# Entry of a two-layer step on one core: norm squares over whole tiles, the order of first loads, and the place of the later modulation groups

## The chip, the cores and the metric

The kernel runs on one core of one Trainium2 chip. TensorE (PE) does the matrix products, ScalarE (ACT) and VectorE (DVE) the elementwise work, GpSimd (POOL) a little of it; SyncE (SP), ACT and POOL issue DMAs. The metric is the device time of one execution in microseconds, lower being better.

## The reference, cut to what matters

Two trunk layers with adaptive layer norm run over 512 latent and 128 context tokens of width 1024. The change lies in the first lines of layer 0: modulation, norm, and the first input projection.

```python
m = jax.nn.silu(cond) @ w_mod + b_mod                      # shift, scale, gate x 2
y = xf * lax.rsqrt(jnp.mean(xf * xf, axis=-1, keepdims=True) + RMS_EPS)
h = y * g * (1.0 + scale) + shift
p = h @ w_in                                               # cq, ckv, krope, nq, nk, nv
cq = rms_norm(cq, q_norm)
```

## The kernel before

Activations lie transposed: eight tiles x[0] to x[7] of 128 x 640, one for each 128 of the width; columns 0 to 319 and 320 to 639 are the left and the right half (a and b in names of results). A product in fp32 precision is made of three fp32r products: the weight's high part with h's high part (h00h), the same with h's residue (h00l), and the weight's residue with h00h. The high part of a weight tile is an ACT copy (L184), its residue a DVE subtraction (L185). So one unit of 128 output rows costs 8 k x 2 halves x 3 = 48 products.

The entry, in the order in which it is written:

- vec (norm gains, biases, conditions) is loaded on SP (L131); ACT makes silu of the conditions (L332, L333) and loads the exponential tables (L159).
- x is loaded by eight DMAs on SP (L495). The class Norm squares each half of each tile on ACT (L211, L214) and adds it up on DVE (L215). rstd sums over partitions with a product against ones (tile n00p) and makes the reciprocal root on ACT.
- fetch(j) loads the weights of modulation group j in two halves of 1 MB (tile mraw, L523); j = 0 to 3 covers the shift and scale of k = 2j and 2j + 1. m[j][0] and m[j][1] are its products (32 in the profile's count, tile mod), m[j][2] a selection (sel, four short products) and the bias add on DVE (L363).
- made(j) does the selection, the gain (gs, L370), and then hm.make for k = 2j and 2j + 1 in both halves: a DVE product (h00t, L241), ACT's high part (h00h, L245), DVE's residue (h00l, L246). The right half is done in two pieces, columns 320 to 511 and 512 to 639, which have different conditions.
- first(ks, us) does the products of units 0, 1 and 2 (weights wA0, wA1, wA4) for some k.

Behind it, lowrank copies the results of units 0 and 1 (cqr) and squares and adds them (cqacc), the tile tabK serves kra and krb on DVE, and wA2 and wA3 give the next unit pair, ckv0 and ckv1. cqp is the norm sum over cqacc on PE. nvp follows with a third kind of products.

Each engine runs its instructions in a fixed order. Program order and a list scheduler at build time set that order; `run` gives each piece the latest product as the point behind which it may be placed. Raw weights pass through three buffers, split weights through three more.

Of the kernel before, what the change touches and what calls it, by code (L numbers as in the profile page):

```python
# [11 lines left out]
F32 = mybir.dt.float32  # L12
F32R = mybir.dt.float32r
AF = mybir.ActivationFunctionType
# [4 lines left out]
P = 128  # L19
D = 1024  # L20
KT = D // P
NS = 512
NP = 128
T = NS + NP
# [26 lines left out]
def body(ctx, tc, xT, vecs, crow, wm0, wm0g, wm1, wA, wNV, wNA, wMK, wMV, wOA, wGQ, wGK, wGV, wOC,  # L51
         wFI, wFO, cckvT, ckrT, cnkT, cnv, cgkT, cgv, rpbp, tabM, tabK, tabG, maskN,
         yT, o_ckvT, o_krT, o_nkT, o_nv, o_gkT, o_gv):
    nc = tc.nc
    V, S, G = nc.vector, nc.scalar, nc.gpsimd

    class PE:

        last = None
# [28 lines left out]
    def bank(name, kind="m"):  # L88
        if kind == "m":
            return psp.tile([P, 512], F32, tag="m", bufs=4, name=name)  # L90
        return ypool["pool"].tile([P, 512], F32, tag=kind, bufs=ypool["tags"][kind], name=name)
# [4 lines left out]
    def pair(name, kind="y"):  # L96
        return [bank(f"{name}a", kind), bank(f"{name}b", kind)]
# [7 lines left out]
    def f(ap):  # L105
        return ap.bitcast(F32)
# [4 lines left out]
    HALF = ((0, HT), (HT, T))  # L111
    HCOND = (((0, HT, 0),), ((HT, NS, 0), (NS, T, 1)))

    def run(pieces):

        for piece in pieces:
            with tc.issue_after(PE.last.ins):
                piece()
# [7 lines left out]
    def named(prefix, pieces):  # L126
        return {f"{prefix}{i}": piece for i, piece in enumerate(pieces)}


    vec = main.tile([P, V_ALL], F32, name="vec")  # L130
    nc.sync.dma_start(vec, vecs)  # L131
    ident = main.tile([P, P], F32, name="ident")
    make_identity(nc, ident)
    ones = main.tile([P, P], F32, name="ones")
# [27 lines left out]
    def load(src, n, name):  # L162
        raw = rawp.tile([P, 1024], F32, tag="raw", name=name)
        nc.sync.dma_start(raw[:, :n], src)
        return raw[:, :n]

    def after(inst, fn):
        if inst is None:
            return fn()
        with tc.issue_after(inst.ins):  # L170
            return fn()
# [3 lines left out]
    def unit(src, n, name, lo="v", pool=None, behind=None, raw=None):  # L175

        if raw is None:
            raw = load(src, n, name + "r")
        elif src is not None:
            nc.sync.dma_start(raw, src)  # L180
        t = (pool or wp).tile([P, 2, 1024], F32R, tag="w", bufs=3, name=name)
        hi, lw = t[:, 0, :n], t[:, 1, :n]
        at = behind if isinstance(behind, tuple) else (behind, behind)
        split[:] = (after(at[0], lambda: S.activation(hi, raw, AF.Copy)),  # L184
                    after(at[1], lambda: (V if lo == "v" else G).tensor_tensor(lw, raw, f(hi), ALU.subtract)))  # L185
        return hi, lw

    def mm3(ps, a, b, h, l, st, sp, **k):
        PE.matmul(ps, a, h, start=st, stop=False, **k)
        PE.matmul(ps, a, l, start=False, stop=False, **k)  # L190
        PE.matmul(ps, b, h, start=False, stop=sp, **k)

    def proj(ps, wh, wl, hh, hl, ks, c0, c1, first=True, last=True, w0=0):

        for j, k in enumerate(ks):
            a, b = wh[:, (w0 + j) * P:(w0 + j + 1) * P], wl[:, (w0 + j) * P:(w0 + j + 1) * P]
            mm3(ps[:, :c1 - c0], a, b, hh[k][:, c0:c1], hl[k][:, c0:c1], first and j == 0, last and j == len(ks) - 1)


    class Norm:  # L200
        last = None
# [165 lines left out]
    def mkgs(l, i, k0=0, k1=8):  # L367
        sc = SC1 if i == 0 else SC2
        n = (V_NMIX if i == 0 else V_NFFN) + 8 * l
        V.scalar_tensor_tensor(gs[l][i][:, k0:k1, :], mods[l][:, sc + k0:sc + k1, :], 1.0, bc2(vec[:, n + k0:n + k1]),  # L370
                               ALU.add, ALU.mult)
# [119 lines left out]
    nrm = Norm("n00", D)  # L491
    x = []
    for k in range(KT):
        xk = ring.tile([P, T], F32, tag="x", name=f"x0_{k}")
        nc.sync.dma_start(xk, xT[:, k, :])  # L495
        x.append(xk)
    for k in range(KT):
        for i in range(2):
            nrm.add(x[k], i)
    hm = Mod("h00", x, gs[0][0], mods[0], SH1, (range(8), range(8)))  # L500
    hh, hl = hm.hh, hm.hl
    cnd = keep.tile([P, 2, KT], F32, name="cnd")
# [5 lines left out]
    nc.gpsimd.dma_start(crs.rearrange("c (k p) -> (c k) p", p=P), cnr[:2 * KT, :])  # L508
    pss = [pair(f"wA{u}") for u in range(2)] + [[bank(f"wA2{c}") for c in range(2)]]

    def first(ks, us):
        for k in ks:
            for u in us:
                for c, (c0, c1) in enumerate(HALF):
                    proj(pss[u][c], *w3[u], hh, hl, [k], c0, c1, first=k == 0, last=k == KT - 1, w0=k)

    with tc.tile_pool(name="start", bufs=1) as big:
        raws = {}

        def fetch(j):  # L520
            for half in range(2):
                raws[j, half] = big.tile([P, 2, 1024], F32, tag="mraw", bufs=8, name=f"mraw{j}_{half}")
                nc.sync.dma_start(raws[j, half], wm0[j, 2 * half:2 * half + 2].rearrange("q p n -> p q n"))  # L523


        fetch(0)
        w3 = [unit(wA[0], 1024, "wA0")]
        fetch(1)
        w3 += [unit(wA[i], 1024, f"wA{i}") for i in (1, 4)]
        fetch(2)  # L530
        fetch(3)
        m = [mod0(j, lambda j=j: bank(f"mod{j}", "m"), lambda j, half: [raws[j, half][:, q, :] for q in range(2)]) for j in range(4)]

        def made(j):

            m[j][2]()
            mkgs(0, 0, 2 * j, 2 * j + 2)
            for k in (2 * j, 2 * j + 1):
                for i in range(2):
                    hm.make(i, nrm.rs, k)  # L540

        def rows(j):
            return m[j][:2]

        nrm.rstd(0)
        run([lambda: nrm.rstd(1)] + rows(0))
        run([lambda: made(0)] + rows(1))
        run([lambda: first((0, 1), [0]), lambda: made(1), lambda: first((0, 1), [1, 2])])
        run(rows(2))
        run([lambda: first((2, 3), [0]), lambda: made(2), lambda: first((2, 3), [1, 2])])  # L550
        run(rows(3))
        run([lambda: first((4, 5), [0]), lambda: made(3), lambda: first((4, 5), [1, 2])])
        run([lambda u=u: first((6, 7), [u]) for u in range(3)])
    sb = ExitStack()
    sa = ExitStack()
    aa = sa.enter_context(tc.tile_pool(name="aa", bufs=1, reuse_waits="tile"))
    ab = sb.enter_context(tc.tile_pool(name="ab", bufs=1, reuse_waits="tile"))

    kr = keep.tile([P, 768], F32, name="kr")
    for q in range(4):  # L560
        nc.scalar.dma_start(kr[32 * q:32 * q + 32, 512:640], ckrT)

    def lowrank(nm, pss):
        ts, nr = [], Norm(nm, 256)
# [47 lines left out]
    pss = [pair(f"ckv{u}") for u in range(2)]  # L612
# [16 lines left out]
    for kk in range(4):  # L629
        wh, wl = wnext  # L630
        for j in range(2):
            k = 2 * kk + j
            a, b = wh[:, 512 * j:512 * (j + 1)], wl[:, 512 * j:512 * (j + 1)]
            for i in range(5):
                c0, c1 = P * i, P * i + P
# [289 lines left out]
    for h in range(8):  # L925
        p, r = divmod(h, 2)
# [8 lines left out]
        qh, ql, ks = [t[r] for t in nqk[p]]  # L935
        pieces = named("s", sc)
# [124 lines left out]
    for h in range(8):  # L1061
        p, r = divmod(h, 2)
# [6 lines left out]
        pieces = named("s", sc)  # L1069
# [758 lines left out]
    x, pend = mixer_out(wOA, oMs + oNs, [4, 5, 6, 7, 0, 1, 2, 3], x_again, mods[0], "oa", nxt, op[-1], begun, scored)  # L1828
# [3 lines left out]
    x, pend = ffn(0, x, pend, box["m"], nxt, side, op)  # L1832


    hh, hl = box2["m"].hh, box2["m"].hl
# [226 lines left out]
    for h in range(8):  # L2062
        oG.append(gp.tile([P, T], F32, tag="go", bufs=8, name=f"oG{h}"))
        pts = []
        pieces = gqa_scores(h, pts)
# [23 lines left out]
    x, pend = mixer_out(wOC, oGs, list(range(8)), lambda n, x=x: x[n], mods[1], "oc", nxt, op[-1], begun, None)  # L2089
# [14 lines left out]
    x, pend = ffn(1, x, pend, box["m"], final, side, op)  # L2104
# [157 lines left out]
```

## Time and profile before

| what | value |
|---|---|
| timed runs | 1481.26, 1482.27 and 1484.97 us, median 1482.27 |
| profiled execution, first to last instruction | 1482.4 us |
| PE busy | 1443.7 us (97%) |
| DVE busy | 1210.9 us (82%) |
| ACT busy | 772.0 us (52%) |
| first product that needs h (wA0) | 24.94 us |
| first product of ckv0a | 53.97 us |
| first product of nvp | 68.89 us |

For the profiled execution the page gives the span alone, 1482.4 us, and no time around it; it lies within the timed runs. In rows of the timeline the first number is the start, the second the length; what follows "<-" in brackets is what ended the idle time before. In the chain of waits each row is a piece of the work that ended last. Windows give pairs of busy time and count for PE, PEld (weight loads), DVE, ACT and POOL, and then the granted clock, the DMA share and GB/s.

### The profile page before, as it was taken

The page shows a single profiled execution, that of the slowest core. Times are in us where ns is not written, and L with a number is a line of the kernel's source. Part 1 is how long each engine was busy: PE and PEld are TensorE (multiplying, and loading weights), DVE is VectorE, ACT ScalarE, POOL GpSimd, SP SyncE. Part 2 cuts the span into 40 slices and gives each one's busy share as a digit, 9 for nine tenths or more (in the row PEclk, how much of TensorE's full clock was granted, in tenths as well). Part 3 has the DMA queues.
Part 4 walks back from the last instruction along what each step waited for, and adds up shares of the span by engine and source line. Part 5 has one row for each costly group of instructions (what it writes and reads, how often), then busy time and mean ns, then how long its engine had stood idle before and what let it go on. Part 6 is the DMA issues. An engine that isn't in the chain of part 4 may idle for free.

```text
span 1482.4 us, 25722 instructions
## 1 busy us (share of the span) xinstructions
PE 1443.7 (97%) x9785; PEld 1394.3 (94%) x9785; DVE 1210.9 (82%) x2278; ACT 772.0 (52%) x1525; POOL 207.0 (14%) x298
## 2 busy tenths in 40 slices
PE   5999989999999999999999999999999999999997
PEld 4988978889999999999999999989999999999996
DVE  5786788886999999977997888775899999954496
ACT  5445677873755444441123666663755555542253
POOL 0226534432000000000001322222000000000000
PEclk9999999999999999999999999999999999999998
DMA  9644511016055555569763211004055556668522
GB/s 368 223 146 138 181 39 43 30 32 211 29 196 171 187 185 183 185 211 344 275 209 128 86 55 46 29 31 135 30 186 177 184 192 206 212 224 308 194 87 72
DMA packets 79900, 228.61 MB, mean 154 GB/s; under 512 B 8864, under 2 KB 14272, under 8 KB 79392
## 3 DMA queue, kind: packets, MB, share of 16 engines
q1 hardware_dynamic: 76832, 219.73, 43.3%
q0 software_dynamic: 1600, 5.14, 1.0%
q10 hardware_dynamic: 1344, 2.10, 0.4%
q8 instruction: 77, 1.26, 0.3%
q14 instruction: 47, 0.39, 0.1%
HBM read 192.23 MB, written 34.69 MB: 153 GB/s over the span
## 4 chain that ended last, share of the span: by engine, by line
PE 83%; DVE 7%; ACT 5%; DMA 2%; issue 2%; POOL 0%; DVEq 0%; ACTq 0%; SPq 0%; POOLq 0%
PE fg L63 21%; PE fd L63 9%; PE fo L63 8%; PE fu L63 6%; PE gq L63 3%; PE nq L63 2%; PE nk L63 2%; PE fo_2b L63 1%; PE fo_0b L63 1%; PE gs L63 1%; PE fo_2a L63 1%; PE fo_0a L63 1%; PE go L63 1%; PE mod L63 1%; PE fo_4b L63 1%
## 5 line engine op out<-in xcount | busy, mean ns | idle before, releaser
L1796 DVE SCALAR_TENSOR_TENSOR junk<-wm,cb 128x1024 bf16<-128x1024 f32 x62 | 75.6, 1220 | 4.6 <-DMA wm<-in_wm 4.1
L1239 ACT ACTIVATE sg<-g 128x320 f32<-128x320 f32 x34 | 16.0, 472 | 114.9 <-DVE g L1239 114.9
L63 PE MATMUL gq<-h10h,wgq 128*128 128x320 f32 x256 | 66.7, 318 | 0.0
L255 POOL TENSOR_SCALAR h10h<-h10t,gs,mods 128x320 fp32r<-128x320 f32 x4 | 3.6, 890 | 429.4 <-DVE h10t L249 427.7
L1239 DVE SCALAR_TENSOR_TENSOR junk<-wm,cb 128x1024 bf16<-128x1024 f32 x50 | 61.0, 1221 | 0.8
L1239 DVE TENSOR_TENSOR wY<-s,wY 128x1024 fp32r<-128x1024 f32 x40 | 48.8, 1220 | 1.1 <-ACT wY L1239 1.0
L1239 DVE TENSOR_TENSOR wZ<-s,wZ 128x1024 fp32r<-128x1024 f32 x40 | 48.8, 1220 | 0.0
L63 PEld LDWEIGHTS gq<-h10h,wgq 128*128 128x128 f32 x256 | 45.0, 188 | 0.9 <-PE gtp L67 0.2
L1239 ACT ACTIVATE wZ<-s 128x1024 fp32r<-128x1024 f32 x40 | 42.4, 1060 | 0.1
L1239 ACT ACTIVATE wY<-s 128x1024 fp32r<-128x1024 f32 x40 | 42.0, 1049 | 0.0
L63 PE MATMUL gq<-h10l,wgq 128*128 128x320 f32 x128 | 39.5, 308 | 0.0
L1978 ACT ACTIVATE gp<-gs,gb,rq 128x640 f32<-128x640 f32 (+1 forms) x40 | 31.9, 797 | 14.5 <-DVE gb L1977 14.1
L63 PE MATMUL fg<-h11E,wW 128*128 128x320 f32 x240 | 38.7, 310 | 0.0
L63 PE MATMUL fg<-h01q,wX 128*128 128x320 f32 x240 | 38.6, 309 | 0.0
L63 PE MATMUL fg<-h11q,wX 128*128 128x320 f32 x240 | 38.6, 309 | 0.0
L63 PE MATMUL fg<-h01N,wZ 128*128 128x320 f32 x240 | 38.6, 309 | 0.0
L63 PE MATMUL fg<-h11N,wZ 128*128 128x320 f32 x240 | 38.6, 309 | 0.0
L63 PE MATMUL fu<-h01q,wX 128*128 128x320 f32 x240 | 38.6, 308 | 0.0
L63 PE MATMUL fu<-h11q,wX 128*128 128x320 f32 x240 | 38.6, 309 | 0.0
L63 PE MATMUL fg<-h01E,wW 128*128 128x320 f32 x240 | 38.6, 309 | 0.0
L63 PE MATMUL fd<-h01q,wZ 128*128 128x320 f32 x240 | 38.5, 309 | 0.0
L63 PE MATMUL fd<-h11q,wZ 128*128 128x320 f32 x240 | 38.5, 309 | 0.0
(3226 smaller groups left out, 5249.6 us busy)
## 6 DMA issues: line engine op xcount, KB each, us to landing
wm<-in_wm SPq DMA_DIRECT2D x48, 512.0 KB, 3.6
mraw<-in_wm SPq DMA_DIRECT2D x8, 1024.0 KB, 15.4
mraw<-in_wm SPq DMA_DIRECT2D x16, 512.0 KB, 3.9
hr_T<-sp_T SPq DMA_DIRECT2D x21, 320.0 KB, 5.9
hr_B<-sp_B SPq DMA_DIRECT2D x18, 320.0 KB, 6.1
mrow<-in_wm0g POOLq DMA_DIRECT2D x8, 512.0 KB, 6.2
wm<-in_wm0g SPq DMA_DIRECT2D x8, 512.0 KB, 3.4
x<-in_xT SPq DMA_DIRECT2D x8, 320.0 KB, 5.7
```

What stands on the lines that cost most here:

```text
L63: cls.last = nc.tensor.matmul(*a, **k)
L255: G.tensor_scalar(h[:, c0:c1], t, self.gsl[:, k, 0:1], self.ml[:, self.sh + k, 0:1], ALU.mult, ALU.add)
L1239: self.last = after(self.last, lambda: op(*a, **k))
L1796: def step(kind, at, line=lambda op, *a, **k: op(*a, **k)):
L1978: weighed.append((S.activation(dst, src, AF.Exp, bias=nb, scale=rq[:, j:j + 1], accum_out=ll[:, j:j + 1]), v))
```

## The change

The diff, with its hunks shortened by nothing but context:

```diff
-    nc.sync.dma_start(vec, vecs)
+    nc.scalar.dma_start(vec, vecs)
+    S.preload_act_table_set("silu_and_others")
...
-    for k in range(KT):
-        for i in range(2):
-            nrm.add(x[k], i)
...
-    def first(ks, us):
+    def first(ks, u):
         for k in ks:
-            for u in us:
-                for c, (c0, c1) in enumerate(HALF):
-                    proj(pss[u][c], *w3[u], hh, hl, [k], c0, c1, first=k == 0, last=k == KT - 1, w0=k)
+            for c, (c0, c1) in enumerate(HALF):
+                proj(pss[u][c], *w3[u], hh, hl, [k], c0, c1, first=k == 0, last=k == KT - 1, w0=k)
...
-        def fetch(j):
+        def fetch(j, half):
+            raws[j, half] = big.tile([P, 2, 1024], F32, tag="mraw", bufs=8, name=f"mraw{j}_{half}")
+            nc.sync.dma_start(raws[j, half], wm0[j, 2 * half:2 * half + 2].rearrange("q p n -> p q n"))
+
+        for k in range(KT - 1):
+            sq = nrm.acc if k == 0 else big.tile([P, T], F32, tag="sq", bufs=2, name=f"n00sq{k}")
+            S.activation(sq, x[k], AF.Square)
+            if k:
+                V.tensor_add(nrm.acc, nrm.acc, sq)
+        nrm.k = [KT - 1, KT - 1]
+        for i in range(2):
+            nrm.add(x[KT - 1], i)
+        for half in range(2):
+            fetch(0, half)
+        w3 = [unit(wA[i], 1024, f"wA{i}") for i in range(2)]
+        for half in range(2):
+            fetch(1, half)
+        w3.append(unit(wA[4], 1024, "wA4"))
+        for j in (2, 3):
             for half in range(2):
-                raws[j, half] = big.tile([P, 2, 1024], F32, tag="mraw", bufs=8, name=f"mraw{j}_{half}")
-                nc.sync.dma_start(raws[j, half], wm0[j, 2 * half:2 * half + 2].rearrange("q p n -> p q n"))
-
-
-        fetch(0)
-        w3 = [unit(wA[0], 1024, "wA0")]
-        fetch(1)
-        w3 += [unit(wA[i], 1024, f"wA{i}") for i in (1, 4)]
-        fetch(2)
-        fetch(3)
+                fetch(j, half)
...
-        def rows(j):
-            return m[j][:2]
-
         nrm.rstd(0)
-        run([lambda: nrm.rstd(1)] + rows(0))
-        run([lambda: made(0)] + rows(1))
-        run([lambda: first((0, 1), [0]), lambda: made(1), lambda: first((0, 1), [1, 2])])
-        run(rows(2))
-        run([lambda: first((2, 3), [0]), lambda: made(2), lambda: first((2, 3), [1, 2])])
-        run(rows(3))
-        run([lambda: first((4, 5), [0]), lambda: made(3), lambda: first((4, 5), [1, 2])])
-        run([lambda u=u: first((6, 7), [u]) for u in range(3)])
+        run([lambda: nrm.rstd(1)] + m[0][:2] + [lambda: made(0)])
+        for j in range(4):
+            k = 2 * j
+            pieces = [lambda: first((k, k + 1), 0), lambda: first((k,), 1), lambda: first((k + 1,), 1), lambda: first((k, k + 1), 2)]
+            if j < 3:
+                pieces[2:2] = [lambda: made(j + 1)]
+                pieces[1:1] = m[j + 1][:2]
+            run(pieces)
...
-    for q in range(4):
-        nc.scalar.dma_start(kr[32 * q:32 * q + 32, 512:640], ckrT)
+    with tc.issue_after(hm.act[KT - 1, 1].ins):
+        for q in range(4):
+            nc.scalar.dma_start(kr[32 * q:32 * q + 32, 512:640], ckrT)
```

The vec load moves to ACT's queue and the table of silu is loaded ahead of its wait. Seven of eight tiles are squared and added whole, the last in halves. The load of wA1 goes ahead of the second modulation group's weights. In each pass the order becomes: unit 0 for both k, the next group's products, unit 1 for the even k, the next group's selection and h, unit 1 for the odd k, unit 2. The four small kr loads go behind the last h on ACT's queue.

How this moves instructions shows at three places. In names, h00h2 is the high part of h for k = 2, h00l2 its residue, wA0a and wA0b the two halves of unit 0, and wA20 and wA21 those of unit 2 (weights wA4).

The first place is PE behind the first modulation group, ahead of the first products with h. Before:

```order
L63 MATMUL mod0_248<-mraw0_1_211,scol_107 32x256 x8
L63 MATMUL mod0_248<-sel_92,modsb0_265 128x4 x2
L63 MATMUL mod1_294<-mraw1_0_218,scol_107 32x256 x8
L63 MATMUL mod1_294<-mraw1_1_220,scol_107 32x256 x8
L63 MATMUL wA0a_200<-h00h0_177,wA0_215 128x320
L63 MATMUL wA0a_200<-h00l0_185,wA0_215 128x320
```

After:

```order
L63 MATMUL mod0_230<-mraw0_1_191,scol_108 32x256 x8
L63 MATMUL mod0_230<-sel_93,modsb0_247 128x4 x2
L63 MATMUL wA0a_157<-h00h0_134,wA0_197 128x320
L63 MATMUL wA0a_157<-h00l0_142,wA0_197 128x320
...
L63 MATMUL wA0b_158<-h00l1_143,wA0_197 128x320
L63 MATMUL wA0b_158<-h00h1_135,wA0_197 128x320
L63 MATMUL mod1_288<-mraw1_0_205,scol_108 32x256 x8
L63 MATMUL mod1_288<-mraw1_1_207,scol_108 32x256 x8
L63 MATMUL wA1a_159<-h00h0_134,wA1_202 128x320
```

The products of modulation group 1 now stand behind all twelve of unit 0 for k = 0 and 1. On DVE, at the same time, the residue of wA1 moves up. DVE before, from the residue of wA0 to that of wA1:

```order
L185 TENSOR_TENSOR wA0_215<-wA0r_213,wA0_215 128x1024
L246 SCALAR_TENSOR_TENSOR h00l0_185<-h00t00_272,mods0_98,h00h0_177 128x320
L241 SCALAR_TENSOR_TENSOR h00t01_276<-x0_0_117,gs00_100,n00rs_116 128x128
L246 SCALAR_TENSOR_TENSOR h00l0_185<-h00t01_276,mods0_98,h00h0_177 128x192
...
L246 SCALAR_TENSOR_TENSOR h00l1_186<-h00t11_287,mods0_98,h00h1_178 128x128
L185 TENSOR_TENSOR wA1_224<-wA1r_222,wA1_224 128x1024
```

After:

```order
L186 TENSOR_TENSOR wA0_197<-wA0r_195,wA0_197 128x1024
L247 SCALAR_TENSOR_TENSOR h00l0_142<-h00t00_254,mods0_99,h00h0_134 128x320
L242 SCALAR_TENSOR_TENSOR h00t01_258<-x0_0_118,gs00_101,n00rs_117 128x128
L186 TENSOR_TENSOR wA1_202<-wA1r_200,wA1_202 128x1024
L247 SCALAR_TENSOR_TENSOR h00l0_142<-h00t01_258,mods0_99,h00h0_134 128x192
```

The residue of wA1 now stands ahead of the right half of k = 0 and of all of k = 1.

The second place is PE between the selection of one group and the first products with its h. Before:

```order
L63 MATMUL mod1_294<-sel_92,modsb1_311 128x4 x2
L63 MATMUL wA1a_202<-h00h0_177,wA1_224 128x320
...
L63 MATMUL wA21_205<-h00h1_178,wA4_229 128x320
L63 MATMUL mod2_376<-mraw2_0_232,scol_107 32x256 x8
L63 MATMUL mod2_376<-mraw2_1_234,scol_107 32x256 x8
L63 MATMUL wA0a_200<-h00h2_179,wA0_215 128x320
```

After:

```order
L63 MATMUL mod1_288<-sel_93,modsb1_305 128x4 x2
L63 MATMUL wA1a_159<-h00h1_135,wA1_202 128x320
...
L63 MATMUL wA21_162<-h00h1_135,wA4_211 128x320
L63 MATMUL wA0a_157<-h00h2_136,wA0_197 128x320
L63 MATMUL wA0b_158<-h00h2_136,wA0_197 128x320
L63 MATMUL wA0a_157<-h00l2_144,wA0_197 128x320
```

Between the selection and h of k = 2 stood 24 products and the next group's 32; now 18 products stand there, and in unit 0 nine of twelve come ahead of the right half of k = 3.

The third place is PE behind the last products of unit 2. Before:

```order
L63 MATMUL wA21_205<-h00l7_192,wA4_229 128x320
L63 MATMUL wA21_205<-h00h7_184,wA4_229 128x320
L63 MATMUL ckv0a_624<-h00h0_177,wA2_614 128x320
L63 MATMUL ckv0a_624<-h00l0_185,wA2_614 128x320
...
L63 MATMUL ckv0a_624<-h00h1_178,wA2_614 128x320
```

After:

```order
L63 MATMUL wA21_162<-h00h7_141,wA4_211 128x320
L63 MATMUL cqp0_706<-cqacc_570,ones_87 128x320
L63 MATMUL ckv0a_606<-h00h0_134,wA2_596 128x320
L63 MATMUL ckv0a_606<-h00l0_142,wA2_596 128x320
L63 MATMUL ckv0b_607<-h00h0_134,wA2_596 128x320
L63 MATMUL ckv0b_607<-h00l0_142,wA2_596 128x320
L63 MATMUL cqp1_712<-cqacc_570,ones_87 128x320
L63 MATMUL ckv1a_608<-h00h0_134,wA3_601 128x320
```

The norm sums cqp moved from behind all of ckv to its front, between products with the high parts of wA2 and wA3. On DVE the residue of wA2 moved behind kra, krb and the cqacc adds, which before it preceded; on ACT the high part of wA2 moved behind all copies and squares of cq.

## The prediction

> **What bounds the kernel now.** I read the page first (span and the chain's shares), then the chain of waits through the entry, then the timeline of each engine there, and last the windows with the granted clock.
>
> ```profile
> span 1482.4 us, 25722 instructions
> PE 83%; DVE 7%; ACT 5%; DMA 2%; issue 2%; POOL 0%; DVEq 0%; ACTq 0%; SPq 0%; POOLq 0%
> ```
>
> PE is on the chain for 83% of the span. Whatever the change does, it does in the first 70 us, and the rest follows as a block as long as PE runs without a gap behind it. The chain there:
>
> ```profile
> 3.08 5.92 DMA x<-in_xT
> 9.02 14.02 DMA mraw<-in_wm
> 23.08 1.94 PE mod L63 x16
> ...
> 26.11 0.80 PE wA0b L63 x3
> ...
> 28.51 0.65 PE mod L63 x4
> ...
> 32.82 1.86 PE mod L63 x32
> ...
> 36.64 0.34 PE mod L63 x4
> ...
> 44.42 0.34 PE mod L63 x4
> ...
> 48.38 0.44 PE wA0a L63 x3
> ...
> 50.05 0.56 PE wA0b L63 x2
> ...
> 52.37 1.76 PE wA L63 x12
> 54.13 3.52 PE ckv0a L63 x24
> ...
> 68.21 1.08 PE cqp L63 x4
> ...
> 104.64 7.05 PE nk L63 x48
> ```
>
> Read from top to bottom: up to 23.08 us the chain waits for DMA (the weights of the second modulation group). From 23.08 to 104.64 + 7.05 = 111.69 us it holds PE alone, so 23.08 us is where the entry ends. Part of what follows ran at half clock:
>
> ```profile
> 22.36:25.77 3.41, 2.69 (x19) 1.43 (x20) 3.41 (x10) 1.78 (x5) 0.66 (x5) 0.50 1.03 412
> 25.77:29.19 3.42, 3.42 (x16) 3.42 (x15) 1.69 (x3) 2.09 (x3) 0.27 (x2) 0.51 1.02 410
> 29.19:54.13 24.94, 24.93 (x206) 22.27 (x207) 17.34 (x49) 12.25 (x30) 3.46 (x11) 1.00 0.60 217
> ```
>
> The last three numbers of a row are granted clock, DMA share and GB/s; the first pair is PE. PE has 24.93 busy of 24.94 us between 29.19 and 54.13: in that stretch nothing is left to gain, only to lose. What can be won lies ahead of 29.19.
>
> **The change part by part.** *1. Start, to the first norm sum on PE.*
>
> ```profile
> 0.74 0.38 SPq L131 DMA_DIRECT2D vec<-in_vecs  x1
> 6.58 5.77 ACT L214 ACTIVATE n00sq<-x 128x320 f32<-128x320 f32 x14
> 8.29 0.67 DVE L144 COPY sel<-ident 32x2 f32<-32x2 f32 x4
> 8.99 4.51 DVE L215 TENSOR_TENSOR n00acc<-n00acc,n00sq 128x320 f32<-128x320 f32 x11
> 13.15 2.50 PE L63 MATMUL n00p<-n00acc,ones 128*128 128x320 f32 x4 [7.89 <-DVE n00acc L215]
> L495 SPq DMA_DIRECT2D x<-in_xT x8: 328/392/432, 1.2 to 5.3; - x8
> DMA to landing us min/median/max: 3.2/5.7/6.3
> ```
>
> Half squares take 5.77 / 14 = 0.41 us each, sixteen 6.6 us, to 12.35. With the table load moved ahead of the wait for vec and the vec load off SP, ACT can begin earlier, but the last x tile is issued at 5.3 and lands near 11.5; one issue less on SP (from 0.74 to the first x issue at 1.2, 0.45 us) makes that 11.05 at best. Whole tiles have no row of their own: an add of 128x320 takes 0.41 us and one of 128x1024 1.22 (row in 2), so I take 0.77 for 640, near the middle. Six whole adds, the small copy (0.67) and the first half add are 5.7 us; with x1 squared about 6.2 and short waits for later tiles they end near 12.8. So the first norm sum moves from 13.15 to about 12.85: **-0.3 us**. Ends: -1.1 (DVE not behind, bound by landing: 11.05 + 0.41 + 0.41 + 0.1 = 12.0) and 0 (landing unchanged).
>
> [...]
>
> *2. First group and second modulation group.* Before, the mod1 products (the second group's 32) run while DVE and ACT still make h for k = 0 and 1, in time in which PE has nothing else. After, PE's order has all 12 wA0 products ahead of them, so mod1 has to wait for the last h of k = 1, and DVE makes that one later, because the residue of wA1 now stands in the middle of k = 0.
>
> ```profile
> 15.58 3.53 PE L63 MATMUL mod<-mraw,scol 128*32 128x256 f32 x32
> 21.59 1.22 DVE L185 TENSOR_TENSOR wA<-wA0r,wA 128x1024 fp32r<-128x1024 f32 x1
> 25.09 1.14 DVE L246 SCALAR_TENSOR_TENSOR h00l<-h00t,mods,h00h 128x320 fp32r<-128x320 f32 x3
> ```
>
> DVE ends k = 1 at 25.09 + 1.14 = 26.23. Minus 0.3, plus 1.2 for wA1's residue, priced as wA0's: 27.1. Two products at half clock (0.27 each, by 0.80 for three at 26.11) put the end of wA0 at 27.6. The 32 mod rows cost 1.86 us at full clock (32.82) and 3.53 at the slow pace of 15.58. If the clock comes back at 29.19 as before, 1.6 us of slow work does 45% of them, the other 55% takes 1.0: 30.2. Then six wA1 products (0.88) and the selection (0.34): 31.4. Before, the same work (12 wA0, mod1, sel1, six wA1) is done at 28.51 + 0.65 + 0.88 = 30.04. **+1.4 us.** Ends: +0.1 (norm 1.1 earlier and the same clock: the 0.8 saved shortens the slow part, then full clock) and +3.0 (clock back one window of 3.41 us later). The load of wA1 ahead of mod1's weights costs nothing: it delays these by 512 KB at 410 GB/s, 1.3 us, to about 24.3, and they are now wanted at 27.6.
>
> [...]
>
> *3. Later groups.* After, the products of a group go wA0 (12), mod rows, six wA1, sel, six wA1, 12 wA4, and then wA0 of the next group. Between sel and the next wA0 lie 18 products; before, 24 products and the 32 mod rows. What has to fit in between:
>
> ```profile
> 41.04 0.75 ACT L245 ACTIVATE h00h<-h00t,mods 128x192 fp32r<-128x192 f32 x2 [1.24 <-DVE h00t L241]
> 41.53 0.68 DVE L246 SCALAR_TENSOR_TENSOR h00l<-h00t,mods,h00h 128x192 fp32r<-128x192 f32 x2 [0.26 <-ACT h00h L245]
> 49.63 0.42 PE L63 MATMUL wA0b<-h00h,wA 128*128 128x320 f32 x1
> 50.05 0.42 PE L63 MATMUL wA0b<-h00l,wA 128*128 128x320 f32 x1
> ```
>
> sel2 ends at 36.64 + 0.34 = 36.98; the last h of that group is there at 41.79 (+4.8), its residue at 42.21 (+5.2). sel3 ends at 44.76 and the last products start at 49.63 and 50.05, again +4.87 and +5.29: here, with 24 products and no mod rows as cover, PE already loses 0.48 us (12 products from 48.38 to 50.05 + 0.56 = 50.61, 2.24 instead of 1.76). After, PE reaches the right half of the odd k after 18 + 9 products, 27 x 0.147 (0.44 for three at 48.38) = 3.96 us behind sel. It waits 0.9 for h, then 0.25 for the residue: 1.1 us, at three boundaries, 3.3, less the 0.48 paid already: **+2.8 us.** Ends: -0.5 (h always there in time) and +3.8 (1.4 each).
>
> *4. Into ckv.* The order changes here too: a cqp norm sum stands first behind wA4, then products with the high part of wA2 and wA3, and the wA2 residue comes after kra, krb and both adds on DVE.
>
> ```profile
> 52.07 1.23 DVE L185 TENSOR_TENSOR wA<-wA2r,wA 128x1024 fp32r<-128x1024 f32 x1 [2.07 <-ACT wA L184]
> 53.44 0.89 DVE L215 TENSOR_TENSOR cqacc<-cqacc,cqsq 128x320 f32<-128x320 f32 x2
> 54.25 0.47 DVE L584 TENSOR_TENSOR kra<-wA,tabK 32x320 f32<-32x320 f32 x1
> 54.74 0.48 DVE L585 TENSOR_TENSOR krb<-wA,tabK 32x320 f32<-32x320 f32 x1
> 0.74 1.83 ACTq L561 DMA_DIRECT2D kr<-in_ckrT  x4
> ```
>
> Call the end of wA4 E (54.13 before, when wA2's residue was long done). kra needs wA4's left half, ready about E - 0.3; kra, krb and the first add are 0.49 + 0.49 + 0.43, so cqp starts at E + 1.15. Behind it on PE are 8 high products and the other cqp (2 x 0.54 + 1.17 = 2.25), to E + 3.4; the residue comes after the second add and two more of kra and krb, E + 1.15 + 0.43 + 0.98 + 1.23 = E + 3.8. Together **+1.5 us**; the cqp work itself only moves forward from 68.21. The four kr loads, now on ACT's queue behind the last h, hold ACT 1.83 us; then follow eight short copies and squares and wA2's high part, near E + 1.3, just hidden by cqp. Ends: +0.4 (adds not held up by kra) and +2.6 (ACT another 1.1 late).
>
> *Sum*, with part 1 inside part 2: 1.4 + 2.8 + 1.5 = **+5.7 us**. The profiled execution has 1482.4 us from first to last instruction; the three timed runs have 1481.26 to 1484.97 with median 1482.27, so the profile stands at the median and I add to 1482.4: **1488.1 us**. I expect nothing back later: PE is without a gap to 111.69, and the DVE work that moves ahead of the nvp products only makes DVE less late.
>
> **Rivals.** (a) *The boundaries are covered.* If the last h came within 3.96 us of sel, part 3 would be -0.48 and the sum 1.4 - 0.5 + 1.5: 1484.8. For it: DVE loses 0.26 and ACT 1.24 us in waits for each other in each group. Against: the +4.8 and +5.2 stand twice in the trace.
>
> (b) *Not slower: the late work is taken back downstream.*
>
> ```profile
> 80.00:90.00 10.00, 10.00 (x45) 8.26 (x44) 10.00 (x18) 2.46 (x4) 0.00 (x0) 1.00 0.57 209
> ...
> 110.00:120.00 10.00, 9.90 (x65) 9.58 (x64) 5.99 (x24) 5.86 (x17) 6.69 (x16) 1.00 0.21 68
> ```
>
> DVE, the third pair, runs at 10.00 of 10 us from 80 to 90; moved-up cq and ckv work could free a later stage that waits for DVE or ACT (they are 12% of the chain). It would have to give back all 5.7 us, giving about 1482; it decides from where DVE, not PE, ends a stage behind 111 us. Against: DVE falls to 5.99 of 10 at 110 to 120, so its backlog is gone by then.
>
> (c) *Clock.* It returns only at 32.6, and part 2 is +3.0: with the rest 1489.7, and with a second loss where PE now idles at E, up to 1491.4 (1.7 us is half a window).
>
> (d) *The change does what its words say and no more:* squares and first weights earlier (-1.1 at the start), cold stretch shorter, boundaries covered: 1482.4 - 1.1 - 1.5, near 1479.8.
>
> **How the numbers follow.** Forecast 58%, (c) 15%, (a) 15%, (b) 8%, (d) 4%. A change of 0.3% (4.4 us) is about what can be told from none: below 1477.9 faster, above 1486.7 slower. Of the forecast, whose own spread is about 1485.5 to 1490.5, some 85% lies above 1486.7; with (c) that is slower 0.64. Faster is the tail of (d) and of (b): 0.03. The rest, 0.33, is the same. The range goes from 1483.0, under (a), to 1491.4, the top of (c); it leaves out (b), (d) and the upper tail.
>
> **What would show it.** Right: the mod1 rows start near 27.6 and not before the 12 wA0 products; idle PE of about 1 us, released by ACT and DVE, ahead of the right half of k = 3, 5 and 7; about 1.2 us ahead of the first cqp, released by the DVE add. Wrong: PE without gaps from 27 to 60, a clock at 1.00 through 22 to 29, or ckv starting before 57 us. The sum fails if nvp, at 69.3 before, starts before 73.

## The result, and the profile after

The changed kernel takes 1494.8 us (median of four runs, 1494.28 to 1497.02), the kernel before 1482.77 us in the same series: ratio 1.0083, 95% interval 1.0071 to 1.0095, **slower by 12.0 us**. The direction was predicted, the size was not: +5.7 us was forecast, and 1494.8 lies above the range, which ended at 1491.4.

The page of after, span and shares of the chain:

```profile
span 1492.8 us, 25704 instructions
...
PE 84%; DVE 8%; ACT 5%; issue 2%; DMA 0%; DVEq 0%; POOL 0%; ACTq 0%; POOLq 0%
```

DMA had 2% of the chain before and has 0% now: the 14.02 us for the weights of the second modulation group are gone from the entry, and so are three later loads near 350 us, 10.8 us together. DVE has a point more, PE too. The chain of waits of after, from the vec load to ckv (start, length, piece):

```profile
0.74 3.52 DMA vec<-in_vecs
...
14.01 2.50 PE n00p L63 x4
...
23.63 1.14 DVE wA L186
24.77 0.59 DVE h00l L247 x2
25.36 0.47 DVE h00t L242
25.83 0.02 issue
25.85 0.57 ACT h00h L246
26.42 0.04 issue
26.47 1.49 PE wA0a L63 x3
27.96 0.80 PE wA0b L63 x3
28.76 3.39 PE mod L63 x32
...
33.22 0.35 PE mod L63 x4
...
38.42 0.41 PE wA0b L63
38.84 0.56 PE wA0b L63 x2
39.40 1.86 PE mod L63 x32
...
61.76 0.24 DVE cqacc L216
62.00 1.09 issue
63.09 0.73 DVE cqacc L216
...
64.86 1.24 DVE wA L186
66.09 0.04 issue
66.14 3.49 PE ckv0a L63 x22
```

Three things are to be seen. Behind the first selection and up to 26.47 the chain runs through DVE and ACT, which make h, the residue of wA1 (23.63) among it; the only DMA left on the chain in the entry is the vec load at its start. The 32 modulation rows take 3.39 us at 28.76 and 1.86 at 39.40. And on the way into ckv there is a DVE addition with 1.09 us of "issue", time in which it waited for nothing that the profile shows.

Four marks on PE sum the two kernels up. "Second selection" is the first product behind the selection of group 1; after has by then done six wA1 products more, 0.88 us of work. The middle column is a second profile of the kernel before, taken for a reason that follows below.

| mark, us from the span's start | before | before, second profile | after |
|---|---|---|---|
| first n00p | 13.15 | 13.25 | 14.01 |
| behind the second selection | 29.02 | 26.71 | 33.42 |
| last product of wA4 ends | 54.13 | 51.90 | 61.16 |
| first nvp | 68.89 | 66.66 | 79.14 |
| span | 1482.4 | 1479.8 | 1492.8 |
| nvp to the end | 1413.5 | 1413.1 | 1413.7 |

From nvp to the end these three profiles differ by no more than 0.6 us. The loss of after lies ahead of nvp.

### The profile page after: what moved, and what is told of

Same layout as the page of the kernel before. It is cut to its first block, busy times and chain, and to the rows that moved or that the text cites. A ratio compares the mean times of both kernels' runs of the same rounds, so it can differ in the third digit from the quotient of the medians.

```text
span 1492.8 us, 25704 instructions
## 1 busy us (share of the span) xinstructions
PE 1447.5 (97%) x9785; PEld 1395.1 (93%) x9785; DVE 1208.2 (81%) x2272; ACT 771.1 (52%) x1518; POOL 208.1 (14%) x298
## 4 chain that ended last, share of the span: by engine, by line
PE 84%; DVE 8%; ACT 5%; issue 2%; DMA 0%; DVEq 0%; POOL 0%; ACTq 0%; POOLq 0%
PE fg L63 21%; PE fd L63 9%; PE fo L63 8%; PE fu L63 6%; PE gq L63 3%; PE nq L63 2%; PE nk L63 2%; PE fo_2b L63 1%; PE fo_0b L63 1%; PE gs L63 1%; PE mod L63 1%; PE fo_0a L63 1%; PE fo_2a L63 1%; PE go L63 1%; PE fo_4b L63 1%
## 5 line engine op out<-in xcount | busy, mean ns | idle before, releaser
L63 PE MATMUL fg<-h01C,wY 128*128 128x320 f32 x240 | 38.5, 309 | 0.0
```

Of the source, the lines that this page charges most:

```text
L63: cls.last = nc.tensor.matmul(*a, **k)
```

## The experiments

The theory was that of the prediction, in three places: second group and clock, later boundaries, the way into ckv; the rivals put all of the loss into one of them. Eleven runs follow, one of them of the kernel before itself. Times are medians, with the ratio to the kernel before and its interval; norm_two_chains and before_again were timed once each. Marks come from one profile of each run.

### One part of the change at a time

**kr_first**: the changed kernel with the kr loads back at their old place.

```diff
-    with tc.issue_after(hm.act[KT - 1, 1].ins):
-        for q in range(4):
-            nc.scalar.dma_start(kr[32 * q:32 * q + 32, 512:640], ckrT)
+    for q in range(4):
+        nc.scalar.dma_start(kr[32 * q:32 * q + 32, 512:640], ckrT)
```

> The changed kernel, but the four kr loads stand where they stood before (at the head of ACT's queue). Built so, cqp goes back behind ckv and the wA2 residue back ahead of kra. Theory (each part of the change has its own price, and the 3.0 us lost between wA4 and nvp belong to the kr loads alone): about 3 us faster than the changed kernel, so +9 us against before; in its profile ckv0a starts right behind wA4. Rival (the kr loads are harmless, PE would wait at that place anyway because cq's copies on ACT are late): +12 as the changed kernel.

**kr_alone**: the same edit the other way round, as the only change to the kernel before.

> The kernel before with one edit: the four kr loads go behind the last h on ACT's queue. Theory: +3 us (2.5 to 3.5), with cqp ahead of ckv, PE idle ahead of the first cqp and the DVE add of cqacc the thing it waits for. Rival (harmless): 0 within 1 us.

**groups_alone**: the kernel before with the new order of groups and products only.

```diff
-        run([lambda: nrm.rstd(1)] + rows(0))
-        run([lambda: made(0)] + rows(1))
...
+        run([lambda: nrm.rstd(1)] + m[0][:2] + [lambda: made(0)])
+        for j in range(4):
+            k = 2 * j
+            pieces = [lambda: first((k, k + 1), 0), lambda: first((k,), 1), lambda: first((k + 1,), 1), lambda: first((k, k + 1), 2)]
+            if j < 3:
+                pieces[2:2] = [lambda: made(j + 1)]
+                pieces[1:1] = m[j + 1][:2]
+            run(pieces)
```

> The kernel before with the new order of the groups' products alone (norm in halves, vec on SP, first loads and kr loads as before). Theory: boundaries 3 x 1.43 less 0.48 = +3.8, and mod1 behind wA0 +1.4 to +3 depending on when the full clock comes back: together +5 to +7 us. Rival (the loss is one of the clock in the first 32 us, and the boundaries' waits are given back later): +3 or less.

**norm_alone**: the kernel before with the start of the change only (vec on ACT's queue, the early table, whole-tile squares and additions).

```diff
-    nc.sync.dma_start(vec, vecs)
+    nc.scalar.dma_start(vec, vecs)
+    S.preload_act_table_set("silu_and_others")
...
+        for k in range(KT - 1):
+            sq = nrm.acc if k == 0 else big.tile([P, T], F32, tag="sq", bufs=2, name=f"n00sq{k}")
+            S.activation(sq, x[k], AF.Square)
+            if k:
+                V.tensor_add(nrm.acc, nrm.acc, sq)
```

> The kernel before with the norm over whole tiles and the vec load on ACT's queue with the early table load; groups, first loads and kr loads as before. Theory: the first norm sum starts 0.5 to 0.9 us later than before (13.15), but PE is waiting for the second group's weights up to 23.08 anyway, so 0 to +0.5 us in time. Rival (a late start goes through to the end): +1 us or more.

The column "half clock" says for how many us ahead of nvp, from 19 us on, the windows show a granted clock of one half: before has 6.8 there, its second profile 3.4, after 10.2.

| run | half clock | n00p | wA4 end | nvp | span | median | ratio (interval) |
|---|---|---|---|---|---|---|---|
| kr_first | 6.8 | 14.57 | 60.90 | 75.66 | 1490.3 | 1493.69 | 1.0077 (1.0060 to 1.0094) |
| kr_alone | 6.8 | 12.98 | 53.34 | 71.35 | 1484.6 | 1487.16 | 1.0031 (1.0020 to 1.0042) |
| groups_alone | 6.8 | 13.15 | 59.03 | 73.78 | 1487.9 | 1489.37 | 1.0045 (1.0030 to 1.0060) |
| norm_alone | 0 | 14.39 | 53.72 | 68.48 | 1484.8 | 1485.02 | 1.0017 (1.0007 to 1.0026) |

Each part costs time alone. The medians stand 4.8, 7.0 and 2.6 us above the 1482.39 of before in that series, 14.4 together, where the whole change costs 12.0. At nvp, against the second profile of before (66.66), groups_alone has +7.1, kr_first 1.9 more (start and first loads) and after another 3.5 (the kr loads): 12.5. As the profiles differ in half clock, each step can hold some of it. norm_alone cost more than the 0 to 0.5 us expected; its profile is of its slowest run (1486.67 us), and the 1416.3 us from nvp to the end are 3.2 more than in the second profile of before.

For one part the medians are weaker than the marks: kr_first's median is only 1.1 us under that of after, with intervals that overlap, though nvp comes 3.5 us and the end of the span 2.5 us earlier; about 3 us were expected. How much of the kr loads' price is left in the whole change is therefore not settled by the times; alone they cost 4.8 us, ratio 1.0031, where 2.5 to 3.5 were expected. Of the 4.8 the rows ahead of nvp show 3.2: from the end of wA4 to nvp kr_alone takes 18.0 us, before 14.8.

Which products follow wA4 depends on the kr loads alone: kr_first has the old order into ckv, and kr_alone, which changes nothing else, the new one.

### What the start does

In norm_alone the first norm sum comes at 14.39 instead of 13.15. DVE's timeline there (the last bracket is the idle time before and who ended it):

```profile
7.44 2.68 DVE L525 TENSOR_TENSOR n00acc<-n00acc,n00sq 128x640 f32<-128x640 f32 x3 [2.50 <-ACT n00sq L523]
10.04 0.67 DVE L145 COPY sel<-ident 32x2 f32<-32x2 f32 x4
10.74 0.28 DVE L505 COPY cnr<-cps 16x128 f32<-16x128 f32 x1
11.05 2.69 DVE L525 TENSOR_TENSOR n00acc<-n00acc,n00sq 128x640 f32<-128x640 f32 x3
13.84 0.89 DVE L216 TENSOR_TENSOR n00acc<-n00acc,n00sq 128x320 f32<-128x320 f32 x2
```

DVE has no idle time from 7.44 on, and ACT waits for it: the additions are the bound, at 2.69 / 3 = 0.90 us a tile. The prediction had priced one at 0.77. My reading was that each addition waits for the one before it, since all go into the same tile. **norm_two_chains** tried it: whole squares, additions in halves, the rest as before.

```diff
+            S.activation(sq, x[k], AF.Square)
+            if k:
+                for c0, c1 in HALF:
+                    V.tensor_add(nrm.acc[:, c0:c1], nrm.acc[:, c0:c1], sq[:, c0:c1])
```

> The kernel before, but the first seven tiles are squared whole (as in the change) while each square is added in halves; the vec load stays on SP and no table is loaded early; all else as before. norm_alone had the first n00p at 14.39 us against 13.15. Theory (the whole-tile adds are one chain in which every add waits for the one before it, 0.92 us a tile): with halves there are two chains again, an add costs about 0.45, and n00p starts at 12.6 to 13.3 us. Rival 1 (the two square buffers make ACT wait for DVE, whatever the adds are): n00p stays at 13.8 us or later. Rival 2 (the late landing of vec on ACT's queue delays the first squares, as silu stands ahead of them): n00p near 13.2 with the adds still in step behind the squares, and the add chain has waits for ACT in it, not the other way round. In all cases the rest of the entry stays within 0.5 us of before, as the second modulation group's weights still bound it: nvp at 68.4 to 69.4 us.

The first n00p started at 14.68 (the one run took 1484.81 us, nvp came at 68.81): the theory of one chain fell, and the number is that of the first rival, though not by its mechanism. The rows:

```profile
8.68 0.49 DVE L525 TENSOR_TENSOR n00acc<-n00acc,n00sq 128x320 f32<-128x320 f32 x1 [0.55 <-ACT n00sq L522]
9.09 0.68 DVE L144 COPY sel<-ident 32x2 f32<-32x2 f32 x4
9.79 0.28 DVE L504 COPY cnr<-cps 16x128 f32<-16x128 f32 x1
10.10 4.03 DVE L525 TENSOR_TENSOR n00acc<-n00acc,n00sq 128x320 f32<-128x320 f32 x9
```

Nine half additions take 4.03 us, 0.45 each, as much for a tile as a whole one; before, eleven took 4.51, 0.41 each. DVE is again without idle time from 8.68 on, so ACT's waits for it follow from DVE being the bound. Why the same half addition takes 0.45 here and 0.41 before stays open. What is shown for norm_alone is where the time is: additions at 0.90 a tile instead of 0.82, the first of them later because a whole square comes first (7.44 instead of 7.07 in before), and the copy cnr (0.28) ahead of the last additions instead of behind them. In norm_two_chains the wait of 0.55 us for a square comes on top.

This delay does not vanish: norm_alone comes to nvp 1.8 us later than the second profile of before, though it has no half clock there. In norm_alone PE waits 0.34 us for the residue of wA1 and again for that of wA4, rows that in the second profile of before had no wait:

```profile
28.62 0.41 PE L63 MATMUL wA1a<-h00h,wA 128*128 128x320 f32 x1 [0.34 <-DVE wA L186]
30.10 0.56 PE L63 MATMUL wA<-h00h,wA 128*128 128x320 f32 x2 [0.34 <-DVE wA L186]
```

### The two orders apart, and the collision on DVE

**group1_back**: kr_first with only the second modulation group again ahead of the first products of unit 0.

```diff
-        run([lambda: nrm.rstd(1)] + m[0][:2] + [lambda: made(0)])
+        run([lambda: nrm.rstd(1)] + m[0][:2])
+        run([lambda: made(0)] + m[1][:2])
...
-                pieces[1:1] = m[j + 1][:2]
+                if j:
+                    pieces[1:1] = m[j + 1][:2]
```

> As kr_first (the changed kernel with the kr loads where they were), and besides the second modulation group's products go back ahead of the first wA0 products; the later groups keep the new order. kr_first starts nvp at 75.66 us in its profile. Theory: mod1 goes back into idle PE time, 1.9 to 3.4 us of products, so nvp starts 2 to 3 us earlier (72.7 to 73.7). Rival (the h of k = 0 and 1 sets the pace whatever stands ahead of it): no more than 0.5 us earlier.

**later_back**: kr_first with the old order for groups 2 and 3.

```diff
+        run([lambda: first((0, 1), 0)] + m[1][:2] + [lambda: first((0,), 1), lambda: made(1), lambda: first((1,), 1), lambda: first((0, 1), 2)])
+        run(m[2][:2])
+        for j in range(2, 4):
+            k = 2 * j - 2
+            run([lambda: first((k, k + 1), 0), lambda: made(j)] + [lambda i=i, u=u: first((i,), u) for i in (k, k + 1) for u in (1, 2)])
```

> As kr_first, and besides the later groups (2 and 3) go back to 24 products and the next group's 32 between a selection and the next wA0; the first group keeps the new order. Theory: two of the three boundaries lose their 1.43 us, and at the last one 0.48 is left: nvp 2.5 to 3.8 us earlier than in kr_first (71.9 to 73.2). Rival (a boundary's wait is only the clock or made up later): under 1 us.

group1_back brings nvp from 75.66 to 72.52 (-3.1 us) and the median to 1489.96, ratio 1.0049 (1.0035 to 1.0063). All of the 3.1 us lies ahead of the second selection, whose mark goes from 33.16 to 30.08. Part of it is clock: kr_first has 6.8 us at half clock there and group1_back none, and the 32 rows of the second group took 3.19 us in kr_first and twice 1.07 in group1_back.

later_back brings nvp to 73.03 (-2.6) and the median to 1490.13, 1.0046 (1.0030 to 1.0061). Its mark behind the second selection is later than that of kr_first, 34.10, with 10.2 us at half clock. From there to the end of wA4 it takes 58.28 - 34.10 = 24.18 us, kr_first 60.90 - 33.16 = 27.74. So the later boundaries cost 3.6 us, more than the 2.6 seen at nvp. With the six products done earlier (0.88) later_back is at 25.06, as before with 25.11: in it the first boundary is covered too, by the 32 rows of group 2, and not two of the three alone, as was expected.

So the second group (with its share of the clock) and the later boundaries both cost, 3 to 4 us each, and neither is all of it.

The boundaries can be read in after itself: from the selection's end (33.22 + 0.35 = 33.57) to the next modulation rows (39.40) are 5.83 us, for 30 products of 0.147, 4.41 us: **1.42 us lost at each of three**. Three of them less the 0.48 that before also loses would be 3.8; later_back shows 3.6.

For the way into ckv, the 1.09 us of "issue" in the chain is read from two timelines of after, DVE and POOL:

```profile
61.76 2.06 DVE L216 TENSOR_TENSOR cqacc<-cqacc,cqsq 128x320 f32<-128x320 f32 x2
```

```profile
61.17 2.94 POOL L764 TENSOR_TENSOR bm<-gt,msk 128x128 f32<-128x128 f32 x6
```

Two additions take 2.06 us instead of 0.89 (the first of them 1.41), and the first cqp waits for them:

```profile
63.32 0.78 PE L63 MATMUL cqp<-cqacc,ones 128*128 128x320 f32 x2 [2.16 <-DVE cqacc L216]
```

POOL is adding up a bias table at that very time, from 61.17 to 64.11. **kr_alone_bias_late** takes kr_alone and makes those sums wait for kr, a value that comes later, by a copy that the sum then overwrites.

```diff
             n1 = n0 + 128
+            if h == 0:
+                G.tensor_copy(bm[0:32, v, o:o + 1], kr[0:32, 0:1])
```

> As kr_alone, with six one-column copies on POOL that make the six bias sums (bm) wait for kr; what they write is written over by these sums. In kr_alone a DVE add of cqacc took 2.08 us for two where before it took 0.89, while POOL ran the bias sums. Theory (the two engines get in each other's way there, DVE's add waits for POOL's sum): the two adds are back at 0.9 us and nvp starts 1.0 to 1.4 us earlier than kr_alone's 71.35. Rival (the adds wait for ACT's squares, not for POOL): adds still end at the same time, nvp unchanged within 0.3 us.

DVE in kr_alone, and then in kr_alone_bias_late:

```profile
53.94 2.08 DVE L215 TENSOR_TENSOR cqacc<-cqacc,cqsq 128x320 f32<-128x320 f32 x2
```

```profile
54.36 0.90 DVE L215 TENSOR_TENSOR cqacc<-cqacc,cqsq 128x320 f32<-128x320 f32 x2
```

With POOL's sums out of the way (they run from 62.14 there) the pair takes 0.90 us. From the end of wA4 to nvp it is 70.58 - 53.76 = 16.8 us instead of 71.35 - 53.34 = 18.0, and the median falls from 1487.16 to 1484.25, ratio 1.0009 (1.0000 to 1.0018). The collision is shown, and costs 1.2 us. nvp itself came only 0.8 us earlier, not 1.0 to 1.4, since wA4 ended 0.4 later. The median fell by more, 2.9 us. In the two profiles 1.5 us lie behind nvp (1484.6 - 71.35 = 1413.25 against 1482.3 - 70.58 = 1411.72), and the granted clock of the whole execution is 0.993 in kr_alone's and 0.995 in the other; whether the edit brings that about is not shown.

### The clock

The profile of before has 6.8 us at half clock. **filled_idle** keeps PE busy there in the kernel before, with 34 idle products ahead of the first norm sum and 13 behind the first selection.

```diff
+                for _ in range(13 if j == 1 and half == 0 and bk.__defaults__ else 0):
+                    PE.matmul(psm[:, 384:512], ones, ones, start=True, stop=True)
...
+    warm = bank("warm")
+    for _ in range(34):
+        PE.matmul(warm[:, :128], ones, ones, start=True, stop=True)
```

> The kernel before with 34 products of ones on ones on PE ahead of the first norm sum and 13 ahead of the second modulation group, all into PSUM columns that nobody reads; nothing else changed. Theory (PE's slow clock in the entry comes from its idle time and costs 3 us of the 31 from 23.08 to 54.13): granted clock 1.00 through 22 to 29, norm sums and the first mod rows at half their time, nvp 2 to 3 us earlier than 68.89, time -2 us or more. Rival (the entry is bound by the weights' landing and by h, the clock costs nothing): within 0.7 us of before.

The clock was 1.00 from 22 to 29 us. The first norm sums took 1.34 us instead of 2.50, but the first 32 rows 3.63 instead of 3.53, with the granted clock at one half from 14.4 to 17.9 us. nvp came at 66.51, 2.4 us earlier than in the profile of before, but the median was 1481.6, ratio 0.9996 (0.9987 to 1.0005): no difference that can be told, where the theory had -2 us or more. So the profile of before seemed to be on the slow side. **before_again** took another, with no edit.

> The kernel before, unchanged, for a second profile of it. Its first profile has span 1482.4 us, which with the 1.8 us that lie around a span in every run here is 1484.2 us, 1.8 above the median of its timed runs. If the cold stretch of the entry has its place by chance, this profile can show another: one window at half clock instead of two, span 1480 to 1481, nvp at 67 to 68 us. If the stretch is fixed by the kernel, it is again two windows from about 22 to 29 us and nvp at 68.9 us, and the 1.8 us stay unexplained.

Its time was 1481.66 us with a span of 1479.8; around the span lie 1.7 to 1.9 us in every run here. The first profile (span 1482.4) thus stands for an execution of about 1484.2 us, not for the median. The windows of the second profile (PE's pair, then PEld, DVE, ACT, POOL, clock, DMA share, GB/s):

```profile
21.00:22.50 1.50, 1.50 (x16) 0.46 (x8) 1.50 (x3) 0.47 (x2) 0.00 (x0) 0.50 1.05 421
22.50:24.00 1.50, 0.97 (x16) 0.44 (x16) 1.50 (x5) 0.86 (x2) 0.00 (x0) 0.52 1.01 401
24.00:25.40 1.40, 1.40 (x18) 0.99 (x11) 1.40 (x5) 1.37 (x5) 0.73 (x5) 1.00 1.04 418
```

Two rows at 0.50 and 0.52, then 1.00 from 24.00 on, where the first profile has 0.51 up to 29.19: the same program, 2.2 us apart at nvp. What sets the length of the stretch is not shown.

**after_filled** does for the changed kernel what filled_idle did for the old one.

```diff
+    def idle(n):
+        for _ in range(n):
+            PE.matmul(pss[1][0][:, 384:512], ones, ones, start=True, stop=True)
...
+                    idle(((8, 0), (3, 0))[k][c])
+                    PE.matmul(ps, a, h, start=k == 0, stop=False)
+                    idle(((4, 5), (1, 0))[k][c])
```

> The changed kernel with 21 idle products (ones by ones, 0.24 us each at full clock, into a spare part of a bank that nothing reads) on PE between the first selection and the first products with h, so that PE is not idle there from 20.3 to 26.5 us. Theory (of the 5.8 us by which the work up to the second selection ends later than in the better profile of before, the half clock from 21.7 to 31.9 us makes about 2): the granted clock stays at 1.00 from 20 to 32, the 32 rows of the second modulation group take 1.86 us instead of 3.39, the second selection starts at 30.6 to 31.4 instead of 33.06, nvp at 76.7 to 77.6 instead of 79.14, and the median is 1492.2 to 1493.5. Rival 1 (the order alone: the last h of k = 1 is what the group waits for, and the clock costs nothing more): the clock stays up and the second selection is still at 32.6 or later. Rival 2 (the clock is all of it): the second selection at 28 to 29 us, nvp near 74, median near 1489.

The windows of after, and then of after_filled, over the same stretch:

```profile
22.40:25.80 3.40, 2.04 (x5) 1.18 (x5) 3.40 (x8) 1.33 (x2) 0.00 (x0) 0.50 1.02 407
25.80:29.20 3.40, 3.25 (x16) 1.99 (x19) 2.92 (x7) 2.15 (x4) 0.00 (x0) 0.50 1.02 407
29.20:32.60 3.40, 3.40 (x35) 1.60 (x28) 0.06 (x1) 0.37 (x1) 0.00 (x0) 0.61 1.02 410
```

```profile
22.40:25.80 3.40, 3.40 (x30) 3.34 (x29) 3.40 (x7) 1.73 (x4) 0.00 (x0) 1.00 1.03 411
25.80:29.20 3.40, 2.95 (x25) 1.94 (x27) 2.92 (x7) 2.15 (x4) 0.00 (x0) 1.00 1.02 408
29.20:32.60 3.40, 3.40 (x40) 2.73 (x33) 0.99 (x5) 0.39 (x1) 0.00 (x0) 1.00 1.03 406
```

The clock stays at 1.00, the second group's rows take 1.86 us (28.60 to 30.46), the second selection starts at 31.38 instead of 33.06, and nvp at 77.47 instead of 79.14: in these profiles the clock is worth 1.7 us of the loss. The median is 1493.52, ratio 1.0071 (1.0057 to 1.0085), at the upper end of what was expected and with an interval that overlaps that of after. The rows still start at 28.53, against 28.69 in after: they wait for h, clock or no clock. That part belongs to the order and to the later h.

No version is faster than before by more than the runs can tell; filled_idle is the only one whose median is not above it.

## Why the size was wrong

| term of the sum | predicted | after against first profile of before | after against second profile |
|---|---|---|---|
| start and second group (parts 1, 2) | +1.4 (+0.1 to +3.0) | 33.42 - 0.88 - 29.02 = +3.5 | +5.8 |
| later boundaries (part 3) | +2.8 (-0.5 to +3.8) | +3.5 | +3.4 |
| into ckv (part 4) | +1.5 (+0.4 to +2.6) | +3.2 | +3.2 |
| at nvp | +5.7 | +10.2 | +12.5 |

**Part 1** had the wrong sign: 14.01 instead of 12.85. Two of its reasons fell. The table load ahead of vec won nothing, since vec landed 3.5 us after its issue on ACT's queue, against 2.1 on SP's, and ACT's first square began at 5.97 (5.85 before). And a whole addition took 0.90 us, not 0.77. The estimate had been put between two rows, 0.41 for 320 columns and 1.22 for 1024, which for 640 is the larger tile's rate; even at the smaller tile's it would have been 0.82.

**Part 2** is the step that failed first: its mechanism was right, its size was not. The 12 wA0 products did come ahead, and the residue of wA1, priced at 1.2 us, stands in the chain with 1.14. But the modulation rows started at 28.69, not 27.6: 1.1 us later, about the 1.16 by which the first norm sum missed part 1. And the step assumed that the clock "comes back at 29.19 as before". It stayed at half for 10.2 us, from 21.6 to near 31.9 (a mean of 0.61 over 29.20 to 32.60 is 2.65 us at half and the rest at full clock), where before had 6.8, and the rows took 3.39 us instead of the 2.6 worked out. The two, 1.9 us, are nearly all of the 2.1 by which the term missed against the first profile. This was rival (c), 15%. The 3.41 us by which the upper end let the clock return later was an estimate from the length of one row of the windows; after has 10.2 us at half clock and before 6.8. For a second loss of 1.7 us behind wA4, where PE idles, which (c) and the top of the range hold, no run shows anything: PE waits 2.16 us there in after, and the granted clock is 1.00 from 32.6 us to nvp. The length of the stretch is in part chance: kr_first, which differs from after by the kr loads alone, has 6.8 us, later_back 10.2. after_filled puts 1.7 us on the clock.

Against the second profile the term is +5.8. Of that groups_alone has 30.22 - 0.88 - 26.71 = 2.6, kr_first 2.9 more (start and first loads; its mark is 33.16) and after another 0.3. The 1.7 of the clock is in these figures, and how it divides among them is open, as the profiles differ in half clock.

**Part 3** held within its range: 1.42 us a boundary against 1.1 predicted and 1.4 as its upper end. The wait ahead of the right half was seen shorter than forecast (0.55 us for h), but the products around it ran apart, 0.41 and 0.27 us instead of 0.147, each released by its own operand. Rival (a), covered boundaries, fell.

**Part 4** had the right place and half the size, beyond its upper end. The first cqp waited 2.16 us where 1.2 was forecast. The residue of wA2 let PE go on 66.14 - 61.16 = 5.0 us behind wA4, not 3.8; the difference is the collision with POOL's bias sums, which the prediction did not look for because POOL stood on no chain. Without it (kr_alone_bias_late) the residue lets PE go on at 57.57 - 53.76 = 3.8, as forecast, and 16.8 us pass to nvp instead of 14.8 in before. Of that +2.05 the prediction had 1.5: it let eight products and two sums cover 2.25 us, where they hold 2.0 (8 x 0.147, and 0.84 from the first cqp to nvp in before), and had no price for the slower products behind a stall or a norm sum (in kr_alone_bias_late from 55.37 to 55.76 and from 56.49 to 56.88, 0.39 us for one, and from 57.57 to 57.97, 0.40 for two, where a run of products has 0.147 each). The kr loads, thought hidden behind cqp, are what brings the new order about: kr_first loses none of the 3.2 us there (14.8 from wA4 to nvp).

Not every DVE instruction was slowed there: beside POOL's sums (61.17 to 64.11) the two cqacc additions, with both inputs in SBUF, took 2.06 us instead of 0.89, while the krb at 61.25, with one input from the matmul's result, took its 0.48. Why the additions and not the krb were slowed is not shown.

**The base** was off by 1.8 us: the prediction took the span as the profile's own time and found it at the median, but the time is 1.8 us longer than the span, and that execution had 6.8 us at half clock in the entry, where the second profile has 3.4. The forecast of 1488.1 misses 1494.8 by 6.7: 2.1, 0.7 and 1.7 from the three terms against the first profile, 1.8 from the base, the rest, 0.4, from behind nvp and from after's median standing 0.25 us above its profiled run (1494.55).

**Rival (b)**, time given back downstream, fell: nvp to the end takes 1413.7 us against 1413.5 and 1413.1. **Rival (d)** fell at the start already. The threshold that the prediction set for its own failure, nvp before 73, was passed on the other side by 6 us. (Its 69.3 for nvp before is the end of the cqp row; the first nvp product starts at 68.89.)

The range missed because two terms lay beyond their own upper ends, parts 1 and 2 with 3.5 against 3.0 and part 4 with 3.2 against 2.6, and because it let at most one term reach its end. All three upper ends together, 9.4 us, would have given 1491.8. The terms share a cause: in all three PE waits for DVE or ACT. In the entry the half clock comes on top; with PE's idle time there filled, after_filled kept 1.00.

## What to carry to other kernels

Work that stands ahead of its operands on an in-order engine must be covered by what is really ready: here the old order had 56 ready instructions between a selection and its h, the new one 18 products, and each boundary lost 1.4 us. When a load is moved "behind" something, look at the order of everything that the scheduler then places differently, on the engines off the chain too: four small loads, moved alone, cost 4.8 us. Take two profiles of a kernel with a stretch at half clock in it before adding small terms to one of them, and add the time around the span.

## What the runs showed of the hardware

- The same program's half-clock stretch in the entry was 6.8 us in one profile and about 3.4 in another, with 2.2 us between them at nvp. From 19 us to nvp the profiles here show 0, 3.4, 6.8 or 10.2 us at half clock, and no other length.
- Early in the kernel the granted clock of the windows does not tell the pace: it reads 1.00 from 13 to 19 us in before, while the first norm sums take 2.50 us there and 1.34 in filled_idle, and 32 rows 3.53 us and later 1.86.
- A DVE addition of two SBUF tiles took 1.41 us beside POOL's additions; 1.09 of it count as issue, longer than two of POOL's (2.94 / 6 = 0.49 us each). DVE went on at 63.09 while POOL still ran to 64.11.
- A DVE copy from one SBUF tile to another, 32 x 512, took 2.31 us instead of 0.43 in the second profile of before, when POOL's sums began beside it; in kr_alone, with POOL's sums done by 56.32, three such copies from 62.09 on took 0.42 to 0.45:

```profile
56.62 0.43 DVE L621 COPY kr<-kr 32x512 f32<-32x512 f32 x1
...
57.45 2.31 DVE L621 COPY kr<-kr 32x512 f32<-32x512 f32 x1
```

```profile
57.40 2.66 POOL L760 TENSOR_TENSOR bm<-gt,msk 128x128 f32<-128x128 f32 x6
```

- The small vec load (79 KB) took 3.5 us from issue to landing on ACT's queue and 2.1 on SP's, and the start gained nothing from the saved issue on SP (ACT's first square at 5.97 us, 5.85 before).
